# A start offset of 88 instead of 192 bytes for split weights that are the stationary side

## The chip, the cores and the metric

The kernel runs on one NeuronCore of a Trainium2 chip. The metric is the device time of one launch in microseconds; lower is better.

## The reference, cut to what matters

One decoder block on 256 tokens of width 1024, in float32. The heavy part is matrix products with large weights:

```python
h = rms_norm(x, g_pre_mix)
proj = h @ w_in          # 1024 x 4256: MoBA q, k, v, MLA latents, 2 x 1024 gate logits
...                      # two attention branches, o_a and o_b
merged = sigmoid(gate_a) * (o_a @ w_branch_a) + sigmoid(gate_b) * (o_b @ w_branch_b)
x = x + rms_norm(merged @ w_out, g_post_mix)
h2 = rms_norm(x, g_pre_mlp)
m = square(relu(h2 @ w_up)) @ w_down      # 1024 -> 4096 -> 1024
x = x + rms_norm(m, g_post_mlp)
```

## The kernel before, in words

Every float32 operand of a large product is split into a high part (`hi`, rounded by ScalarE to the type float32r that TensorE multiplies) and the rest (`lo`, on VectorE: the value minus `hi`). `mm3` (L180 to L185) then makes one product as three matmuls into the same PSUM tile: hi times hi (L182), and the two mixed ones (L185). In a call `nc.tensor.matmul(ps, a, b)` the operand `a` is the stationary side: its 128 columns are first loaded into the array (a row "PEld LDWEIGHTS" in the profile). The operand `b` is the moving side, which is streamed through (a row "PE MATMUL"). The profile names both as out<-moving,stationary. The load for the next matmul runs while the present one streams.

Weights play either part:

- As the **moving** side, 512 columns or so wide, in `a_chunk` (the q, k, v and latent projections), in `mix` (w_out), and in the first four tiles of w_up. There activations are the stationary side.
- As the **stationary** side in `b_tile` and `nope`: 128 columns of a weight are loaded and 256 tokens are streamed. These are the gate logits (`gate_tiles`, names `acc<-xt_hi,whi` and its two companions), part of the MLA projections (`nope`, `acc<-ct_hi,whi`), the two branch projections (`wk<-o_hi,whi`) and w_up from its fifth tile on (`wk<-x_hi,u_hi`).

Each weight block comes from HBM by one DMA on SyncE's queue into a `raw` tile. `halves_of` (first half of the kernel, buffers `whi`, `wlo`) or `split` (MLP, buffers `u_hi`, `u_lo` and others) turn it into `hi` and `lo`. Both functions take a `skew` in bytes. The buffer is 512 bytes longer per partition than the weights need (`ROW // 4` floats), and the weights begin `skew` bytes into it. Callers whose weights become the stationary side pass `SKEW`, all others 0. In the built program every one of these buffers, and the tiles `xt_hi`, `xt_lo`, `ct_hi`, `ct_lo`, `o_hi`, `o_lo`, `x1_hi`, `x1_lo` that are the moving side against them, begins at a multiple of 512 bytes, and so does each 128-column slice of 512 bytes within a block.

TensorE's instructions stand in the order of the program. During the attention part, `weave` puts gate tiles and MLA products between the attention steps. In the MLP, pair i of w_up tiles (48 matmuls of 256 columns) is followed by the w_down products of pair i - 3 (21 or 24 matmuls of 512 columns, where hidden activations `m_hi`, `m_lo` are the stationary side, at skew 0). Buffers for split weights are double in the MLP and five deep before it. In the last two pairs of w_down the `u` buffers are used without a skew, for weights on the moving side.

Of the kernel before, what the change touches and what calls it, by code (L numbers as in the profile page):

```python
# [37 lines left out]
QUOTA_A, QUOTA_B = 1900, 1900  # L38


ROW, SKEW = 512, 192

PLAIN = (0, 5, 10, 14, 15)

# [895 lines left out]
```

## Time and profile before

| | |
|---|---|
| median of 3 runs (lowest to highest) | 364.34 us (364.11 to 364.54) |
| the profiled execution: its time, its span | 365.11 us, 363.4 us |
| TensorE matmul busy | 354.2 us, 97% of the span, 2319 instructions |
| TensorE weight loads busy | 319.0 us, 88% |
| VectorE busy | 297.7 us, 82% |
| ScalarE busy | 247.7 us, 68% |
| mean granted TensorE clock | 0.993 of 2.4 GHz |

The span is the time from the first to the last instruction of the profiled execution; 1.7 us of its time lie around it. Matmuls are pipelined: one that streams 256 columns is recorded as 0.28 us long, yet the next one starts about 0.118 us after it. So what a matmul costs is read from the distance between starts, and not from its own length.

### The profile page before, as it was taken

How to read it: one execution, taken by the hardware profiler on the slowest of the kernel's cores; microseconds unless marked ns; L12 is line 12 of the kernel's file. 1: busy time of each engine (PE TensorE's matmuls, PEld its weight loads, DVE VectorE, ACT ScalarE, POOL GpSimd, SP SyncE). 2: the span in 40 equal slices, each digit the busy share in tenths (PEclk: the TensorE clock that was granted, in tenths of full speed). 3: DMA queues.
4: the chain of work that ended last, by engine and by line, in shares of the span. 5: the costliest groups of instructions: out<-in, count | busy, mean ns of one | idle time of the engine just before them, and what ended most of it. 6: DMA issues, size and time to landing. Idle time of an engine off the chain costs nothing.

```text
span 363.4 us, 6070 instructions
## 1 busy us (share of the span) xinstructions
PE 354.2 (97%) x2319; PEld 319.0 (88%) x2319; DVE 297.7 (82%) x557; ACT 247.7 (68%) x377; POOL 6.1 (2%) x28
## 2 busy tenths in 40 slices
PE   8999999999999999999999999999999999999992
PEld 4899888989989999998888999999999999999881
DVE  3888998885766576795878799998998999989566
ACT  5799779996758755646369977748556777656422
POOL 6000000000000000000000000000000000000000
PEclk9999999999999999999999999999999999999997
DMA  7987872455333355528804656446755655530002
GB/s 266 336 346 258 262 267 91 147 202 175 119 114 119 115 175 185 190 90 341 347 8 133 223 224 215 178 188 231 250 213 199 239 170 206 231 117 0 2 0 115
DMA packets 14604, 66.20 MB, mean 182 GB/s; under 512 B 1648, under 2 KB 1776, under 8 KB 10480
## 3 DMA queue, kind: packets, MB, share of 16 engines
q1 hardware_dynamic: 14256, 65.30, 50.8%
q10 hardware_dynamic: 288, 0.52, 0.4%
q8 instruction: 18, 0.29, 0.3%
q14 instruction: 10, 0.08, 0.1%
q0 software_dynamic: 32, 0.00, 0.0%
HBM read 64.77 MB, written 1.05 MB: 181 GB/s over the span
## 4 chain that ended last, share of the span: by engine, by line
PE 89%; ACT 5%; DVE 3%; DMA 1%; issue 0%; SPq 0%; DVEq 0%; ACTq 0%
PE acc L185 30%; PE wk L185 25%; PE acc L182 15%; PE wk L182 13%; PE wk L367 2%; PE wk L488 1%; DMA raw<-in_weights 1%; ACT u_hi L655 1%; PE wk L520 1%; ACT sq L243 1%; DVE u_lo L656 1%; DVE y L898 1%; ACT x_sb L779 1%; PE wk L489 1%; ACT t_hi L655 0%; PE wk L519 0%
## 5 line engine op out<-in xcount | busy, mean ns | idle before, releaser
L177 DVE TENSOR_TENSOR wlo<-raw,whi 128x1024 fp32r<-128x1024 f32 (+4 forms) x60 | 66.4, 1107 | 16.9 <-ACT whi L177 16.8
L177 ACT ACTIVATE whi<-raw 128x1024 fp32r<-128x1024 f32 (+4 forms) x60 | 57.4, 965 | 24.7 <-PE acc L185 11.5
L185 PE MATMUL wk<-x_hi,u_lo 128*128 128x256 f32 x224 | 62.7, 280 | 0.0
L182 PE MATMUL wk<-x_hi,u_hi 128*128 128x256 f32 x224 | 62.6, 279 | 0.0
L185 PE MATMUL wk<-x_lo,u_hi 128*128 128x256 f32 x224 | 62.5, 279 | 0.0
L185 PEld LDWEIGHTS wk<-x_lo,u_hi 128*128 128x128 f32 x224 | 42.1, 188 | 0.5
L182 PEld LDWEIGHTS wk<-x_hi,u_hi 128*128 128x128 f32 x224 | 41.9, 187 | 0.5
L185 PEld LDWEIGHTS wk<-x_hi,u_lo 128*128 128x128 f32 x224 | 42.0, 188 | 0.0
L655 ACT ACTIVATE u_hi<-raw_u 128x2048 fp32r<-128x2048 f32 (+1 forms) x17 | 31.0, 1826 | 14.1 <-PE wk L185 13.9
L656 DVE TENSOR_TENSOR u_lo<-raw_u,u_hi 128x2048 fp32r<-128x2048 f32 (+1 forms) x17 | 36.8, 2163 | 4.3 <-ACT u_hi L655 4.3
L182 PE MATMUL acc<-xt_hi,whi 128*128 128x256 f32 x128 | 37.4, 293 | 0.0
L185 PE MATMUL acc<-xt_hi,wlo 128*128 128x256 f32 x128 | 35.7, 279 | 0.0
L185 PE MATMUL acc<-xt_lo,whi 128*128 128x256 f32 x128 | 35.7, 279 | 0.0
L805 ACT ACTIVATE m_hi<-m 128x896 fp32r<-128x896 f32 (+1 forms) x16 | 14.7, 927 | 23.5 <-DVE m L801 21.1
L656 DVE TENSOR_TENSOR t_lo<-t,t_hi 128x2048 fp32r<-128x2048 f32 x11 | 25.2, 2291 | 3.9 <-ACT t_hi L655 3.9
L655 ACT ACTIVATE t_hi<-t 128x2048 fp32r<-128x2048 f32 x11 | 21.1, 1916 | 5.7 <-DVE t L843 5.7
L182 PEld LDWEIGHTS acc<-xt_hi,whi 128*128 128x128 f32 x128 | 24.0, 188 | 1.1 <-issue 1.0
L185 PEld LDWEIGHTS acc<-xt_lo,whi 128*128 128x128 f32 x128 | 24.0, 188 | 0.1
L185 PEld LDWEIGHTS acc<-xt_hi,wlo 128*128 128x128 f32 x128 | 24.0, 188 | 0.0
L656 DVE TENSOR_TENSOR b_lo<-raw_d,b_hi 128x1536 fp32r<-128x1536 f32 x11 | 19.3, 1753 | 0.0
L185 PE MATMUL acc<-t_hi,m_lo 128*128 128x512 f32 x46 | 18.0, 392 | 0.5 <-DVE m_lo L806 0.5
L182 PE MATMUL acc<-t_hi,m_hi 128*128 128x512 f32 x46 | 17.9, 390 | 0.0
(254 smaller groups left out, 925.6 us busy)
## 6 DMA issues: line engine op xcount, KB each, us to landing
raw<-in_weights SPq DMA_DIRECT2D x42, 512.0 KB, 3.4
raw_u<-in_weights SPq DMA_DIRECT2D x17, 1024.0 KB, 4.9
raw_d<-in_weights SPq DMA_DIRECT2D x15, 1024.0 KB, 5.3
raw<-in_weights SPq DMA_DIRECT2D x14, 384.0 KB, 4.6
x_sb<-in_x SPq DMA_DIRECT2D x2, 512.0 KB, 7.0
g_post<-in_g_post SPq DMA_DIRECT2D x2, 512.0 KB, 5.4
raw<-in_weights SPq DMA_DIRECT2D x2, 432.0 KB, 8.1
out<-y SPq DMA_DIRECT2D x2, 256.0 KB, 2.0
```

The costliest lines, as they stand in the source:

```text
L177: last_split[:] = nc.scalar.activation(hi, raw, AF.Copy), nc.vector.tensor_tensor(lo, raw, hi, op=OP.subtract)
L182: nc.tensor.matmul(ps, a_hi, b_hi, start=first, stop=False)
L185: nc.tensor.matmul(ps, a, b, start=False, stop=last and i == 1)
L243: return nc.scalar.activation(sq[:, :src.shape[-1]], src, AF.Square, scale=scale, accum_out=accum)
L367: nc.tensor.transpose(ps[:n, i * P:(i + 1) * P], b, ident)
L488: nc.tensor.matmul(o[:, 0:S], v_of(0, h), pts[h][:, 0:S], start=True, stop=False)
L489: nc.tensor.matmul(o[:, P:S], v_of(1, h), pts[h][:, S:S + P], start=False, stop=True)
L520: nc.tensor.matmul(sp[:, P:3 * P], q[:, P:2 * P], k, start=True, stop=True)
L655: ops = nc.scalar.activation(hi[:, c], src[:, c], AF.Copy), \
L656: nc.vector.tensor_tensor(lo[:, c], src[:, c], hi[:, c], op=OP.subtract)
L779: nc.scalar.activation(x_sb[:, t], x_sb[:, t], AF.Copy, scale=unit_inv[:, t:t + 1])
L805: nc.scalar.activation(hi, m[:, used], AF.Copy)
```

## The change

One constant is changed. Hi and lo weights that are the stationary side begin 88 instead of 192 bytes into their buffers. Buffer sizes and places, the order and the number of instructions on every engine, and all DMAs stay as they are. What differs is the start address of the ScalarE and VectorE writes of those halves, and of the weight loads that read them.

```diff
-ROW, SKEW = 512, 192
+ROW, SKEW = 512, 88
```

The lines that use it, unchanged:

```python
hi, lo = (wts.tile([P, UNIT + ROW // 4], F32R, name=n, tag=n)[:, skew // 4:skew // 4 + raw.shape[-1]]
          for n in ("whi", "wlo"))                                        # L175, in halves_of
hi = mlp(f"{tag}h").tile([P, size], F32R, ...)[:, skew // 4:skew // 4 + n]  # L651, in split; L652 for lo
```

## Rows read from the trace of the kernel before

**Rows 1.** The page's head: busy time by engine with its share of the span, and the chain of work that ended last, by engine.

```profile
span 363.4 us, 6070 instructions
PE 354.2 (97%) x2319; PEld 319.0 (88%) x2319; DVE 297.7 (82%) x557; ACT 247.7 (68%) x377; POOL 6.1 (2%) x28
PE 89%; ACT 5%; DVE 3%; DMA 1%; issue 0%; SPq 0%; DVEq 0%; ACTq 0%
```

**Rows 2.** Matmuls by line and operands, in the view of groups that keeps shapes apart: count, busy us, mean ns of one. These are the matmuls whose stationary side begins at the skew: w_up, gates, branch projections, MLA projections. Each stands for three groups of the same count.

```profile
L182 PE MATMUL wk<-x_hi,u_hi 128*128 128x256 f32 x224 | 62.6, 279 | 0.0
...
L182 PE MATMUL acc<-xt_hi,whi 128*128 128x256 f32 x128 | 37.4, 293 | 0.0
...
L182 PE MATMUL wk<-o_hi,whi 128*128 128x256 f32 x64 | 17.9, 280 | 0.0
...
L182 PE MATMUL acc<-ct_hi,whi 128*128 128x256 f32 x20 | 5.9, 293 | 0.0
```

**Rows 3.** The timeline of TensorE: start us, length us, engine, line, operands. First and last of a run of 48 matmuls of one w_up pair, and the first of what follows.

```profile
213.97 0.28 PE L182 MATMUL wk<-x_hi,u_hi 128*128 128x256 f32 x1
214.08 0.28 PE L185 MATMUL wk<-x_lo,u_hi 128*128 128x256 f32 x1
...
219.50 0.28 PE L185 MATMUL wk<-x_hi,u_lo 128*128 128x256 f32 x1
219.62 0.40 PE L182 MATMUL wk<-b_hi,m_hi 128*128 128x512 f32 x1
```

**Rows 4.** The same view, of a run of 330 matmuls (gates and branch projections) without a pause: the second, the last, and what follows; 329 distances lie between the first row and the last.

```profile
122.12 0.28 PE L185 MATMUL acc<-xt_lo,whi 128*128 128x256 f32 x1
...
160.76 0.28 PE L185 MATMUL wk<-o_hi,wlo 128*128 128x256 f32 x1
160.87 0.40 PE L182 MATMUL acc<-whi,mg_hi 128*128 128x512 f32 x1
```

**Rows 5.** The same view, of three shorter runs of the same kind of matmul. Between the rows of each piece lie 9, 15 and 15 distances.

```profile
62.25 0.28 PE L185 MATMUL acc<-ct_hi,wlo 128*128 128x256 f32 x1
...
63.27 0.28 PE L185 MATMUL acc<-ct_hi,wlo 128*128 128x256 f32 x1
...
89.93 0.28 PE L185 MATMUL acc<-xt_hi,wlo 128*128 128x256 f32 x1
...
91.63 0.28 PE L185 MATMUL acc<-xt_hi,wlo 128*128 128x256 f32 x1
...
119.19 0.28 PE L185 MATMUL acc<-xt_hi,wlo 128*128 128x256 f32 x1
...
120.89 0.28 PE L185 MATMUL acc<-xt_hi,wlo 128*128 128x256 f32 x1
```

**Rows 6.** The same view, of matmuls of 256 columns whose stationary side (hidden activations `m`) begins at a multiple of 512 bytes, as the moving side does. 21 distances lie between the two rows.

```profile
353.52 0.28 PE L185 MATMUL wk<-u_lo,m_hi 128*128 128x256 f32 x1
...
356.04 0.28 PE L185 MATMUL wk<-u_lo,m_hi 128*128 128x256 f32 x1
```

**Rows 7.** The same view, of matmuls of 512 columns with the same start of both sides; 17 distances lie between the two rows.

```profile
341.05 0.39 PE L182 MATMUL acc<-b_hi,m_hi 128*128 128x512 f32 x1
...
344.90 0.39 PE L185 MATMUL acc<-t_lo,m_hi 128*128 128x512 f32 x1
```

**Rows 8.** One piece of the chain of work that ended last: start us, length us, and eight transposes (128 columns loaded and 128 streamed each).

```profile
43.29 0.87 PE wk L367 x8
```

**Rows 9.** The timeline of weight loads in one of the runs of rows 5: start us, length us.

```profile
89.94 0.19 PEld L182 LDWEIGHTS acc<-xt_hi,whi 128*128 128x128 f32 x1
90.05 0.19 PEld L185 LDWEIGHTS acc<-xt_lo,whi 128*128 128x128 f32 x1
```

**Rows 10.** Busy us of each engine in stretches (length, then engine busy and count, granted clock, DMA share, GB/s).

```profile
60.00:122.00 62.00, 62.00 (x494) 56.41 (x492) 45.52 (x137) 50.45 (x120) 0.00 (x0) 1.00 0.42 138
122.00:162.00 40.00, 40.00 (x335) 39.81 (x336) 29.88 (x41) 22.60 (x33) 0.00 (x0) 1.00 0.50 162
208.00:340.00 132.00, 131.51 (x857) 120.37 (x857) 124.16 (x126) 88.26 (x77) 0.00 (x0) 1.00 0.51 184
234.80:245.20 10.40, 10.40 (x70) 9.59 (x69) 10.33 (x10) 5.20 (x5) 0.00 (x0) 1.00 0.49 197
```

**Rows 11.** Waits between 208 and 340 us: who waited for whom, us in total, times, longest.

```profile
ACT u_hi L655 <- PE wk L185: 13.9, 8, 3.6
DVE u_lo L656 <- ACT u_hi L655: 3.2, 3, 1.8
DVE m_lo L806 <- ACT m_hi L805: 0.5, 1, 0.5
```

**Rows 12.** Lines 257 and 258, ScalarE and VectorE reading 256 floats from `raw` (at its start) or from `front` (37 floats into the tile): duration ns min/median/max.

```profile
L257 ACT ACTIVATE xt_hi<-raw,front x7: 500/510/513, 6.5 to 12.1; 128x256 fp32r<-128x256 f32 x7
L257 ACT ACTIVATE xt_hi<-front x1: 507/507/507, 3.1 to 3.1; 128x256 fp32r<-128x256 f32 x1
L258 DVE SCALAR_TENSOR_TENSOR xt_lo<-raw,front,xt_hi x7: 478/481/483, 7.0 to 13.1; 128x256 fp32r<-128x256 f32 x7
L258 DVE SCALAR_TENSOR_TENSOR xt_lo<-front,xt_hi x1: 483/483/483, 3.6 to 3.6; 128x256 fp32r<-128x256 f32 x1
```

## The prediction

> **What bounds the kernel now.** I read the page's head first: TensorE's matmuls are busy for 97% of the span, and 89% of the chain that ended last is theirs [rows 1]. The stretches say the same where the change acts: TensorE is busy 62.00 of 62.00 us, 40.00 of 40.00 and 131.51 of 132.00 [rows 10]. So time per matmul is time of the kernel, unless another engine steps in behind it.
>
> Next I counted the matmuls that the change touches, in the view of groups. The four kinds stand three times each: 3 x (224 + 128 + 64 + 20) = 1308 of 2319 matmuls [rows 2]. Their recorded length of 279 ns is no price, since they overlap. The price is the distance between starts, so the timeline comes third. One w_up pair takes 219.62 - 213.97 = 5.65 us for 48, which is 117.7 ns each [rows 3]; the long run of gates and branch projections takes 160.87 - 122.12 = 38.75 us for 329, which is 117.8 ns [rows 4]. 1308 x 117.8 ns = 154 us, 42% of the span. One nanosecond on each is 1.3 us. The measurement of this kernel can tell about 0.2%, or 0.7 us, from no change; that is 0.55 ns per matmul.
>
> **What the start of the stationary side does to that distance, as far as the trace shows it.** Three prices stand in this one profile, all for 256 streamed columns at the full granted clock:
>
> - 120.0 ns where the stationary side begins at a multiple of 512 bytes: 2.52 us for 21 distances [rows 6].
> - 117.7 to 117.8 ns at 192 bytes, in nearly all runs [rows 3, 4].
> - 113.3 ns, also at 192 bytes, in three short runs: 1.02 us for 9, 1.70 us for 15, 1.70 us for 15 [rows 5].
>
> With 512 columns the distance is 3.85 us for 17, or 226.5 ns [rows 7]. So 256 more columns cost 226.5 - 120.0 = 106.5 ns, which is pure streaming. What a matmul pays beyond that is 13.5 ns without a skew, 11.2 ns in the usual state at 192 bytes, and 6.8 ns in the better one. A load starts with each matmul and runs while it streams: a matmul starts at 89.93 us, a load at 89.94 [rows 5, 9]. I read the extra as the load and the stream getting into each other's way, by an amount that hangs on where the two stand relative to each other. That the same addresses give 117.7 in one run and 113.3 in another, each kept for a whole run, says that a small shift at a run's entry is enough to change it. That the load is what disturbs the stream is my inference; the prices are measured.
>
> **The change part by part.** It removes and adds no instruction and moves none, on any engine or queue. Three things get another start address.
>
> *The writes of hi and lo* by ScalarE and VectorE begin 88 bytes into the buffer. No row shows a write at such a place. The nearest are reads of 256 floats that begin 37 floats (148 bytes) into a tile: 507 ns against 510 at a tile's start on ScalarE, 483 against 481 on VectorE [rows 12]. I take nothing, with a bound of 3 ns either way on each of the 41 splits that have the skew (27 before the MLP, 14 of w_up) on each of two engines, 0.2 us, most of it beside TensorE's work.
>
> *The weight loads* read from there. The price per matmul can lie anywhere that the extra can. Below: the extra falls towards nothing until the load itself is the limit. Eight transposes, which load 128 columns but stream only 128, take 0.87 us, or 108.8 ns each [rows 8]; so 109 ns is the floor. Above: 120.0 ns, the price without a skew. A load of 512 bytes that begins 88 bytes in also covers nine pieces of 64 bytes instead of eight, where 192 covers eight; if the extra goes by pieces, the top is 106.5 + 13.5 x 9/8 = 121.7 ns. The present price lies near the upper end of the span from 109 to 121.7: two thirds of it lie below 117.7. A shift of the load against the stream, which 88 bytes surely is, is therefore more likely to lower the price than to raise it. As the value I take 113.3 ns, the one better state that this trace shows.
>
> *The sum.* Of the 1308, some 45 already run at 113.3 (the three runs of [rows 5] have 12, 17 and 16) and about 20 open a stretch after a wait and have another price. 1243 x (117.75 - 113.3) ns = 5.5 us less. From the profiled execution's 365.11 us (span 363.4 and 1.7 around it) that gives 359.6; it lies 0.8 us above the median of 364.34, so the median should be 358.8 us, 1.5% less.
>
> *Does the gain arrive?* In the MLP, VectorE is the cover that could run out. Between 208 and 340 us it is busy 124.16 of 132.00 us, and 576 touched matmuls lie there (three groups of 192), worth 2.6 us; 129.4 us would remain, and VectorE's work still fits. Locally it is tight: one pair has VectorE busy 10.33 of 10.40 us [rows 10], while that pair would shrink by 48 x 4.45 ns = 0.21 us. What saves it is the lead: the split of the next weights waits for TensorE to give its buffer free, 13.9 us in 8 waits of up to 3.6 us, whereas TensorE's stationary activations were late by 0.5 us once [rows 11]. Four such pairs in a row use up 0.6 us or so of that lead. If the lead were gone, the MLP's 2.6 us would shrink to about 1 us and the time would be 360.4. Before 162 us VectorE and ScalarE have 10 us or more to spare in each stretch [rows 10].
>
> The Trainium skill, in "SBUF — State Buffer", section "A bandwidth-pool intuition that's wrong (but worth ruling out)", gives TensorE a second, independent read port for weight loads. By that the load and the stream never meet, and the start address would change nothing: 364.3 us. The trace does not agree: 120.0 and 117.7 ns differ by the start alone [rows 3, 6].
>
> **The rivals.**
>
> *Nothing changes: 364.3 us.* If only the piece of some hundred bytes in which the load begins decides, or the state is set at each run's entry by what came before, 88 bytes could give the same mixture of 117.7 and 113.3. For it: over all the MLP runs the price is the same although the buffers stand at different places. Against it: the step from 0 to 192 bytes did move the price by 2.3 ns, and 0.55 ns would be seen.
>
> *Slower: the load meets the stream as often as without a skew, or more.* The price goes to 120.0 ns: 1243 x 2.25 ns + 45 x 6.7 ns = 3.1 us more, 367.4 us. With the ninth piece, at 121.7 ns, it is 1243 x 3.95 + 45 x 8.4 = 5.3 us more, 369.6. The place is every run of rows 3 and 4; it decides as soon as the price passes 118.3 ns. For it: 88 bytes is no multiple of 16, 32 or 64, while 0 and 192, whose prices are known, are; and it lies nearer to 0, the bad start, than 192 does. Against it: 120.0 is only 2.3 ns above today's price, so there is little room upwards.
>
> The Trainium skill's same page, section "Door 1: The DMA port swizzle (why `[64,N]` ≈ `[32,N]`)", tells of 16-byte lines and of a penalty for each access that crosses to a new one. A load from byte 88 touches 33 such lines and one from 192 touches 32; by that rule this rival holds, at an estimated 11.2/32 = 0.35 ns per matmul, or 364.8 us. No row here begins a load inside such a line, so nothing yet bears it out.
>
> *Much faster: the extra nearly vanishes.* At 109 ns, 1243 x 8.75 + 45 x 4.3 ns = 11.1 us less, 353.3 us. VectorE's cover in the MLP would then be used up (576 x 8.75 = 5.0 us of a slack of 7.8, with no lead left), so I expect 354 to 355 rather than that.
>
> **How the numbers follow.** The better state, 113 ns or near it: 0.40, with a range of its own from 356.5 to 362 (115.9 to 111.5 ns). Much faster: 0.13. No change: 0.14. Slower: 0.33, mostly up to 368. So faster by over 0.2% has 0.53, within 0.2% 0.14, slower 0.33. For the range I leave out the outer half of "much faster" and the tail of "slower" past 368: 354.5 to 368.0.
>
> **What would show it.** Right: the distances in the w_up runs (48 in 5.65 us before) become 48 in 5.44 us, the run of 330 shrinks from 38.75 to 37.3 us, the groups of `u_hi`, `whi` drop from 279 to 276 ns, and VectorE's busy time stays at 298 us. The 120.0 and 226.5 ns of rows 6 and 7 stay, since their starts do. Wrong: distances of 118.3 ns or more; or distances that drop while TensorE gets new waits for `u_lo` or `m_lo` in the MLP; or splits on ScalarE and VectorE that take longer than before.

## The result and the profile after

The changed kernel takes 361.9 us (median of 6 runs, 361.2 to 362.5) against 364.49 us for the kernel before beside it. The ratio is 0.9924, 95% interval 0.991 to 0.9938: 2.6 us faster, where 5.5 us were forecast (358.8 from 364.34). The direction was right; less than half of the size came, and the time lies inside the stated range.

The head of the page after, which answers to [rows 1]: span, then busy time by engine.

```profile
span 360.7 us, 6070 instructions
PE 351.2 (97%) x2319; PEld 315.8 (88%) x2319; DVE 297.6 (82%) x557; ACT 248.1 (69%) x377; POOL 6.1 (2%) x28
```

TensorE's busy time falls by 3.0 us, the span by 2.7; the other engines do what they did. The groups of [rows 2], after:

```profile
L182 PE MATMUL wk<-x_hi,u_hi 128*128 128x256 f32 x224 | 62.2, 278 | 0.0
...
L182 PE MATMUL acc<-xt_hi,whi 128*128 128x256 f32 x128 | 37.4, 292 | 0.0
...
L182 PE MATMUL wk<-o_hi,whi 128*128 128x256 f32 x64 | 17.9, 279 | 0.0
```

The w_up group shrinks by 1 ns on the mean, and the others hardly. The timeline of TensorE (start us, length us, engine, line, operands) shows where they differ. First the run of 48 w_up matmuls that answers to [rows 3]:

```profile
213.41 0.28 PE L182 MATMUL wk<-x_hi,u_hi 128*128 128x256 f32 x1
213.53 0.28 PE L185 MATMUL wk<-x_lo,u_hi 128*128 128x256 f32 x1
213.64 0.28 PE L185 MATMUL wk<-x_hi,u_lo 128*128 128x256 f32 x1
213.76 0.28 PE L182 MATMUL wk<-x_hi,u_hi 128*128 128x256 f32 x1
213.88 0.28 PE L185 MATMUL wk<-x_lo,u_hi 128*128 128x256 f32 x1
...
218.75 0.28 PE L185 MATMUL wk<-x_hi,u_lo 128*128 128x256 f32 x1
218.87 0.40 PE L182 MATMUL wk<-b_hi,m_hi 128*128 128x512 f32 x1
```

218.87 - 213.41 = 5.46 us for 48, where it was 5.65. The first four distances are still 0.12 us; from the fifth on, 113.3 ns: (218.75 - 213.88)/43. Now the run of 330 gates and branch projections that answers to [rows 4], its second, its last and what follows:

```profile
121.98 0.28 PE L185 MATMUL acc<-xt_lo,whi 128*128 128x256 f32 x1
...
160.25 0.28 PE L185 MATMUL wk<-o_hi,wlo 128*128 128x256 f32 x1
160.37 0.40 PE L182 MATMUL acc<-whi,mg_hi 128*128 128x512 f32 x1
```

38.39 us for 329 is 116.7 ns. It fell by 1.1 ns, not by 4.5. And the first run of w_up matmuls after the transposes of L866, 72 of them, takes a third price:

```profile
198.72 0.28 PE L185 MATMUL wk<-x_lo,u_hi 128*128 128x256 f32 x1
...
207.12 0.28 PE L185 MATMUL wk<-x_hi,u_lo 128*128 128x256 f32 x1
207.24 0.40 PE L182 MATMUL acc<-t_hi,m_hi 128*128 128x512 f32 x1
```

8.52 us for 71 is 120.0 ns, where it was 117.8. So at 88 bytes the same kind of matmul costs 113.3, 116.7 or 120.0 ns, each kept through a run, at a granted clock of 1.00. Summed from starts over all 1308 touched matmuls, waits at the heads of runs included:

| runs of touched matmuls | before, us | after, us | change | forecast |
|---|---|---|---|---|
| 12 runs of 48 (w_up) | 67.81 | 65.53 | -2.28 | -2.56 |
| one of 72, one of 24 (w_up) | 11.39 | 11.46 | +0.07 | -0.43 |
| one of 330 (gates, branches) | 38.97 | 38.61 | -0.36 | -1.47 |
| 19 short ones (306 matmuls, among attention) | 37.86 | 37.49 | -0.37 | -1.07 |
| sum, before rounding | 156.04 | 153.09 | -2.95 | -5.5 |

The forecast column is the prediction's 4.45 ns for each matmul it counted, laid out over the runs.

### The profile page after: what moved, and what is told of

Its sections match the earlier page's. It is cut to its first block, busy times and chain, and to the rows that moved or that the text cites. A ratio compares the mean times of both kernels' runs of the same rounds, so it can differ in the third digit from the quotient of the medians.

```text
span 360.7 us, 6070 instructions
## 1 busy us (share of the span) xinstructions
PE 351.2 (97%) x2319; PEld 315.8 (88%) x2319; DVE 297.6 (82%) x557; ACT 248.1 (69%) x377; POOL 6.1 (2%) x28
## 4 chain that ended last, share of the span: by engine, by line
PE 87%; ACT 5%; DVE 4%; DMA 1%; issue 1%; SPq 0%; DVEq 0%; ACTq 0%
PE acc L185 29%; PE wk L185 25%; PE acc L182 15%; PE wk L182 13%; PE wk L367 2%; PE wk L488 1%; ACT u_hi L655 1%; DMA raw<-in_weights 1%; PE wk L520 1%; ACT sq L243 1%; DVE u_lo L656 1%; DVE y L898 1%; ACT x_sb L779 1%; DVE wlo L177 1%; PE wk L489 1%
## 5 line engine op out<-in xcount | busy, mean ns | idle before, releaser
L182 PE MATMUL wk<-x_hi,u_hi 128*128 128x256 f32 x224 | 62.2, 278 | 0.0
L185 PE MATMUL wk<-x_hi,u_lo 128*128 128x256 f32 x224 | 62.1, 277 | 0.0
L185 PE MATMUL wk<-x_lo,u_hi 128*128 128x256 f32 x224 | 62.0, 277 | 0.0
L182 PEld LDWEIGHTS wk<-x_hi,u_hi 128*128 128x128 f32 x224 | 42.1, 188 | 0.5
L185 PEld LDWEIGHTS wk<-x_lo,u_hi 128*128 128x128 f32 x224 | 42.1, 188 | 0.5
L185 PEld LDWEIGHTS wk<-x_hi,u_lo 128*128 128x128 f32 x224 | 42.0, 188 | 0.0
L182 PE MATMUL acc<-xt_hi,whi 128*128 128x256 f32 x128 | 37.4, 292 | 0.0
L185 PE MATMUL acc<-xt_hi,wlo 128*128 128x256 f32 x128 | 35.6, 278 | 0.0
L185 PE MATMUL acc<-xt_lo,whi 128*128 128x256 f32 x128 | 35.6, 278 | 0.0
L182 PEld LDWEIGHTS acc<-xt_hi,whi 128*128 128x128 f32 x128 | 24.1, 188 | 1.1 <-issue 1.0
L185 PEld LDWEIGHTS acc<-xt_lo,whi 128*128 128x128 f32 x128 | 24.1, 188 | 0.1
L185 PEld LDWEIGHTS acc<-xt_hi,wlo 128*128 128x128 f32 x128 | 24.0, 188 | 0.0
L185 PE MATMUL acc<-t_hi,m_lo 128*128 128x512 f32 x46 | 18.0, 392 | 0.4 <-DVE m_lo L806 0.4
L182 PE MATMUL acc<-t_hi,m_hi 128*128 128x512 f32 x46 | 17.9, 390 | 0.0
```

Of the source, the lines that this page charges most:

```text
L182: nc.tensor.matmul(ps, a_hi, b_hi, start=first, stop=False)
L185: nc.tensor.matmul(ps, a, b, start=False, stop=last and i == 1)
```

## The experiments

Theory A, formed from the trace after: the price of a matmul is one of a few states. A run of like matmuls falls into one of them within its first few, by how it is entered, and stays there. The start offset decides which states there are and which one a given entry leads to. Rivals: the gain is spread evenly (B); the offset's place in 64 bytes or in 512 decides alone (C); the dear runs are dear because of their own operands and buffers (D); or the entry alone decides, at any offset (E). In the scans below the lines stand one further down, L183 and L186 for L182 and L185.

**Only the MLP at 88 bytes.**

```diff
-        w = split(load(f"up{2 * i}", "u"), "u", behind, max(len(behind), 1), SKEW)
+        w = split(load(f"up{2 * i}", "u"), "u", behind, max(len(behind), 1), 88)
```

> Only the w_up pairs of the MLP begin at 88 bytes; gates, branch and MLA projections keep 192. Theory A (the price per matmul is a state that is set where a run of matmuls begins, and the start offset only decides which states there are): the twelve runs of 48 w_up matmuls take 5.46 us each as in the changed kernel (5.65 before), the run of 72 stays at 120 ns or falls into another state, and the long run of gates and branches is back at 117.8 ns; together 2.0 to 2.5 us less than before, ratio 0.993 to 0.995. Rival B (the gain is spread evenly over all touched matmuls, about 2.3 ns each): 672 of 1308 matmuls give half of the 2.6 us, ratio 0.9965.

Ratio 0.9948 (0.993 to 0.9966). All twelve runs of 48 take 5.46 us, the run of 72 stays at 120.0 ns, and the run of 330 is back at 117.8 ns.

**Only the part before the MLP at 88 bytes.**

```diff
-ROW, SKEW = 512, 192
+ROW, SKEW = 512, 88
...
-        w = split(load(f"up{2 * i}", "u"), "u", behind, max(len(behind), 1), SKEW)
+        w = split(load(f"up{2 * i}", "u"), "u", behind, max(len(behind), 1), 192)
```

> The other half: gates, branch and MLA projections begin at 88 bytes, the w_up pairs keep 192. Theory A: the w_up runs are back at 5.65 us, the long run of 330 matmuls stays near 116.7 ns or falls into one of the other states seen at 88 bytes (113.3 or 120), and the whole is 0.4 to 1.0 us faster than before, ratio 0.997 to 0.999. Rival B: half of the gain, ratio 0.9965.

Ratio 0.9983 (0.9974 to 0.9993). The w_up runs are back at 5.65 us, the run of 330 is at 116.7 ns. The two halves add up: 0.52% and 0.17% for 0.76% together, within their intervals. B falls: its ratio of 0.9965 for either half lies outside the second interval (just inside the first), and the distances are not spread evenly, 4.0 ns less per matmul in the w_up runs and 1.1 in the run of 330.

**A price for each offset: three scans.** The twelve w_up runs of 48 are all entered alike, after w_down matmuls of 512 columns, and give the same time to 0.01 us. So each can carry an offset of its own, and one kernel prices twelve.

```diff
+SCAN = (0, 64, 128, 192, 256, 320, 384, 448, 24, 88, 152, 216)
...
-        w = split(load(f"up{2 * i}", "u"), "u", behind, max(len(behind), 1), SKEW)
+        w = split(load(f"up{2 * i}", "u"), "u", behind, max(len(behind), 1), SCAN[i - 4] if i >= 4 else SKEW)
```

> Everything at 192 bytes but the twelve w_up pairs 4 to 15, which begin at 0, 64, 128, 192, 256, 320, 384, 448, 24, 88, 152, 216 bytes in this order, one offset for a pair. All are entered alike, after w_down matmuls of 512 columns, so that each run of 48 gives the price of its offset. Theory A with a period of 64 bytes: the first eight do not differ in their states, and 24, 88, 152 and 216 all settle at 113.3 ns. Theory C (the place within 512 bytes counts, as the step from 0 to 192 suggests): 0 is 120 ns, 192 is 117.7, 88 is 113.3 after a few matmuls, and 24, 152 and 216 differ from 88. Within either, the 192 pair must give 5.65 us and the 88 pair 5.46.

> As the scan before, with 8, 16, 32, 40, 48, 56, 72, 80, 96, 104, 112, 120 bytes for the pairs 4 to 15. If the place within 16-byte lines matters (one more line for a load that begins inside one), 8, 40, 56, 72, 104 and 120 are dearer than their neighbours 16, 32, 48, 80, 96 and 112. If only the distance between load and stream matters, the price is smooth or jumps between the few states seen so far (113.3, 116.7, 117.8, 120 ns), whatever the offset within 16 bytes.

> The twelve w_up pairs 4 to 15 begin at 4, 12, 68, 76, 84, 92, 100, 136, 168, 232, 264, 344 bytes. The scans so far: 0 and 256, 64 and 320, 128 and 384, 192 and 448 agree in pairs, so that a period of 256 bytes predicts 264 as 8 (5.56 us) and 344 as 88 (5.46 us). If 88 is the bottom of a smooth valley, 84 and 92 lie at 113 to 116 ns; if the states jump, they are as dear as 80 and 96 (118.6 and 117.4 ns).

Four of the 36 runs, as the timeline has them: first matmul and the one that follows the run, at 0, 88, 76 and 84 bytes. The first two stand in the first scan, the others in the third. The three kernels took 364.78, 365.01 and 364.51 us, one run each.

```profile
212.93 0.28 PE L183 MATMUL wk<-x_hi,u_hi 128*128 128x256 f32 x1
...
218.69 0.40 PE L183 MATMUL wk<-b_hi,m_hi 128*128 128x512 f32 x1
...
308.17 0.28 PE L183 MATMUL wk<-x_hi,u_hi 128*128 128x256 f32 x1
...
313.63 0.40 PE L183 MATMUL acc<-t_hi,m_hi 128*128 128x512 f32 x1
```

```profile
244.60 0.28 PE L183 MATMUL wk<-x_hi,u_hi 128*128 128x256 f32 x1
...
250.05 0.40 PE L183 MATMUL wk<-b_hi,m_hi 128*128 128x512 f32 x1
...
254.85 0.28 PE L183 MATMUL wk<-x_hi,u_hi 128*128 128x256 f32 x1
...
260.61 0.39 PE L183 MATMUL acc<-t_hi,m_hi 128*128 128x512 f32 x1
```

5.76, 5.46, 5.45 and 5.76 us for 48. All of them, as us for the run of 48, from the starts to 0.01 us:

| offsets in bytes | us for 48 |
|---|---|
| 0, 256 | 5.75, 5.75 |
| 64, 320, 192, 448 | 5.65, 5.65, 5.65, 5.65 |
| 128, 384 | 5.77, 5.77 |
| 24, 152, 216 | 5.83, 5.60, 5.74 |
| 88, 344 | 5.46, 5.46 |
| 8, 264 | 5.56, 5.56 |
| 16, 32, 48, 80, 96, 112 | 5.68, 5.68, 5.68, 5.69, 5.63, 5.75 |
| 40, 56, 72, 104, 120 | 5.71, 5.65, 5.68, 5.65, 5.72 |
| 4, 12, 68, 76, 84, 92, 100 | 5.67, 5.61, 5.68, 5.45, 5.76, 5.68, 5.75 |
| 136, 168, 232 | 5.66, 5.76, 5.68 |

Offsets 256 bytes apart give the same, in all six pairs. Within 256 bytes there is no slope to follow: 76 and 88 are the cheapest, and 80, 84 and 92 beside them cost 5.68 to 5.76. C falls in its form of 64 bytes (24 and 88 differ by 0.37 us), and its 512 bytes are 256. That the offset decides alone fell already with the runs of 330 and 72, which have other prices at the same 88 bytes. Beginning inside a 16-byte piece is no mark of a dear offset: 8, 76 and 88 do so and are the cheapest.

Theory A's few states are too simple. At 0, 64, 76, 88, 192 and 216 bytes the distances become even, within about 1 ns of their mean, but at most of the other offsets they go round in a cycle: 112 and 121 ns in turn at 12 bytes, 118, 118 and 124 at 100. At 24 bytes a cycle of seven runs from 117 to 131 ns; a piece of it from the first scan:

```profile
300.71 0.29 PE L186 MATMUL wk<-x_hi,u_lo 128*128 128x256 f32 x1
300.84 0.30 PE L183 MATMUL wk<-x_hi,u_hi 128*128 128x256 f32 x1
300.97 0.28 PE L186 MATMUL wk<-x_lo,u_hi 128*128 128x256 f32 x1
301.09 0.28 PE L186 MATMUL wk<-x_hi,u_lo 128*128 128x256 f32 x1
301.21 0.28 PE L183 MATMUL wk<-x_hi,u_hi 128*128 128x256 f32 x1
```

The mean of a cycle can lie elsewhere than the states, 115.5 ns at 8 bytes and 118.3 at 16. A pattern, even or in a cycle, then stays to the end of the run.

**The entry changed, the addresses kept.** Two matmuls of 512 columns are put in, one at the head of the branch projections, one ahead of the run of 72.

```diff
+        if m == 0: nc.tensor.matmul(ps, o_hi[:, 0, 0, :P], flat(o_hi[:, 0, 0:2]), start=True, stop=True)
...
+            if i == WARM // 2 and j:
+                nc.tensor.matmul(acc_tile(), x1_hi[:, 0, :P], flat(x1_hi[:, 0:2]), start=True, stop=True)
```

> The changed kernel with two matmuls more: each streams 512 columns over a stationary side that begins at a multiple of 512 bytes, as the w_down matmuls do ahead of every w_up run, and writes a tile that is written over or not read. One stands at the head of the branch projections, inside the run of 330 matmuls at 116.7 ns; the other ahead of the run of 72 w_up matmuls at 120 ns. No address of the others changes. Theory A (the state is set by how a run is entered): both runs settle at 113.3 ns; some 310 x 3.3 + 70 x 6.7 ns = 1.5 us less for 2 x 0.23 us more, so about 1.0 us faster than the changed kernel, ratio to the kernel before 0.989 to 0.990. Rival D (these runs are dearer because of their own operands and buffers): 116.7 and 120 ns stay, the kernel is 0.5 us slower than the changed one, ratio 0.994.

The timeline of this kernel around the two:

```profile
123.70 0.39 PE L623 MATMUL wk<-o_hi 128*128 128x512 f32 x1
123.93 0.28 PE L182 MATMUL wk<-o_hi,whi 128*128 128x256 f32 x1
...
159.30 0.40 PE L182 MATMUL acc<-whi,mg_hi 128*128 128x512 f32 x1
```

```profile
197.48 0.48 PE L864 MATMUL acc<-x_hi 128*128 128x512 f32 x1
197.80 0.28 PE L182 MATMUL wk<-x_hi,u_hi 128*128 128x256 f32 x1
...
205.96 0.40 PE L182 MATMUL acc<-t_hi,m_hi 128*128 128x512 f32 x1
```

35.37 us for 312 and 8.16 us for 72: 113.4 ns each, where the same matmuls at the same addresses took 116.7 and 120.0. D falls. The kernel takes 361.15 us, ratio 0.9896 (0.9879 to 0.9912). Beside it on the same chip the changed kernel was run again:

> The changed kernel once more, beside the others on the same chip: ratio 0.991 to 0.994, w_up runs of 5.46 us, the run of 330 at 116.7 ns and that of 72 at 120 ns if the states are the same in every execution.

361.69 us, ratio 0.9915 (0.9901 to 0.993). Its states are those of the first execution: 5.46 us, 38.60 us for the run of 330, 120.0 ns in the run of 72. From the first gate of the long run to w_out it is 37.80 us with the extra matmul against 38.61 (121.50 to 159.30, 121.14 to 159.75), and 8.48 against 8.72 in the run of 72, extra matmul included: 1.0 us less, as expected. In the medians 0.5 us of it shows. The two intervals do not tell that from nothing; all four times of this kernel lie below all four of the other, by as little as 0.04 us.

**The same entry at 192 bytes.**

```diff
-ROW, SKEW = 512, 88
+ROW, SKEW = 512, 192
```

> The kernel before (192 bytes) with the same two extra matmuls as in the entry experiment. Theory A: the offset decides which price a run takes after such an entry, 113.3 ns at 88 bytes and 117.8 ns at 192, so both runs stay at 117.8 ns and the kernel is 0.5 us slower than before. Rival E (the entry alone does it, whatever the offset): the run of 312 and the run of 72 settle at 113.3 ns at 192 bytes too, 1.7 us less.

Both runs stay where they were, as the row of what follows shows against the start of the run of 312 (123.58 us): 36.75 us, 117.8 ns. The run of 72 is at 117.7 ns, the one time 364.52 us. E falls: in these two runs offset and entry decide together.

```profile
123.58 0.28 PE L182 MATMUL wk<-o_hi,whi 128*128 128x256 f32 x1
...
160.33 0.40 PE L182 MATMUL acc<-whi,mg_hi 128*128 128x512 f32 x1
```

**The moving side shifted instead.**

```diff
-    x1_hi = keep.tile([P, KD, S], F32R, name="x1_hi", tag="xt_hi")
+    x1_hi = keep.tile([P, KD * S + 128], F32R, name="x1_hi", tag="xt_hi")[:, 106:106 + KD * S].rearrange("p (k s) -> p k s", s=S)
...
-        w = split(load(f"up{2 * i}", "u"), "u", behind, max(len(behind), 1), SKEW)
+        w = split(load(f"up{2 * i}", "u"), "u", behind, max(len(behind), 1), 0)
```

(`x1_lo` alike; `xt_hi` and `xt_lo` keep their start in buffers of the same new size, and the `u` buffers lose their 512 bytes more.)

> The kernel before, but in the MLP the w_up weights begin at 0 and the moving side x1_hi, x1_lo begins 424 bytes (minus 88, modulo 512) into its buffer, so that the distance between load and stream is that of the changed kernel while the load begins at a multiple of 512 bytes. If only the distance between the two counts, the runs of 48 settle at 113.3 ns (5.46 us). If the place of the load by itself counts, they stay at 120 ns (5.75 us), as 0 bytes gave in the scan. Another price between 113 and 122 ns would say that both places count.

The first run of 48 and the row that follows it:

```profile
213.90 0.28 PE L182 MATMUL wk<-x_hi,u_hi 128*128 128x256 f32 x1
...
219.65 0.39 PE L182 MATMUL wk<-b_hi,m_hi 128*128 128x512 f32 x1
```

All twelve runs of 48 take 5.76 us, 120.0 ns settled, as an offset of 0 with an unshifted moving side does; the one time is 366.24 us, against 364.86 for the kernel before. So the distance between the two sides alone does not set the price: the place of the load counts by itself at this entry. It is one place of the moving side, and whether its start matters while the load begins at 88 bytes was not tried.

**The offset on matmuls of 512 columns.** On top of the entry experiment, the stationary activations of w_out begin at 88 bytes.

```diff
-    mg_hi = late.tile([P, KD, S], F32R, name="mg_hi", tag="m0")
+    mg_hi = late.tile([P, KD * S + 128], F32R, name="mg_hi", tag="m0")[:, 22:22 + KD * S].rearrange("p (k s) -> p k s", s=S)
```

(`mg_lo` alike.)

> The entry experiment (88 bytes, two extra matmuls) with one thing more: the stationary side of the 96 matmuls of w_out (mg_hi, mg_lo), which stream 512 columns, begins 88 bytes into its buffer. If the extra of 13.3 ns belongs to the load's place also where it has twice the time, their distance falls from 226.7 ns to about 220 ns, 0.6 us less in all, ratio to the kernel before about 0.988. If the extra is another thing with 512 columns, it stays at 226.7 ns and the ratio at 0.9896.

The timeline of w_out in this kernel:

```profile
162.63 0.39 PE L182 MATMUL acc<-whi,mg_hi 128*128 128x512 f32 x1
...
175.93 0.39 PE L182 MATMUL acc<-whi,mg_hi 128*128 128x512 f32 x1
```

13.30 us for 57 is 233.3 ns, against 226.7 before: dearer by 6.6 ns, so neither of the two expected outcomes. Ratio 0.9918 (0.9904 to 0.9932). An offset that is among the cheapest for 256 columns is dearer than 0 for 512. The run of 72, behind the same extra matmul, also took 116.7 ns here instead of 113.3: the matmul just ahead of a run does not settle its state alone.

**76 bytes everywhere.**

```diff
-ROW, SKEW = 512, 192
+ROW, SKEW = 512, 76
```

> All stationary split weights begin at 76 bytes, which in the scan settled at 113.3 ns like 88. The w_up runs of 48 take 5.45 us. Theory A says nothing certain of the run of 330 and the run of 72, which are entered otherwise: each takes one of a few prices between 113.3 and 120 ns, and it need not be the one that 88 bytes takes there (116.7 and 120). If it does take 113.3 in both: ratio 0.988; if 120 in both: 0.995.

360.23 us, ratio 0.989 (0.9872 to 0.9908). The same kernel once more, with more runs:

> 76 bytes once more with more rounds. If the states repeat as they did at 88 bytes: the run of 330 at 113.3 ns (37.5 us with its head), the w_up runs at 5.45 us, ratio to the kernel before 0.988 to 0.990, below the interval of the changed kernel (0.9901 to 0.993).

360.77 us, ratio 0.9899 (0.9881 to 0.9918), with the same times in every run of matmuls to 0.02 us. The first execution's page head, long run and first run of 48:

```profile
span 358.6 us, 6070 instructions
PE 348.9 (97%) x2319; PEld 313.4 (87%) x2319; DVE 297.3 (83%) x557; ACT 248.1 (69%) x377; POOL 6.1 (2%) x28
```

```profile
120.99 0.28 PE L185 MATMUL acc<-xt_lo,whi 128*128 128x256 f32 x1
...
158.28 0.40 PE L182 MATMUL acc<-whi,mg_hi 128*128 128x512 f32 x1
...
211.32 0.28 PE L182 MATMUL wk<-x_hi,u_hi 128*128 128x256 f32 x1
...
216.78 0.40 PE L182 MATMUL wk<-b_hi,m_hi 128*128 128x512 f32 x1
```

37.29 us for 329 is 113.3 ns, and the run of 72 settles at 113.3 too. At this offset every run of 12 matmuls or more reaches the cheap state, most within two to seven matmuls, whatever its entry. The touched matmuls take 151.1 us against 156.0: 4.9 us less, and about 4 us less in the medians. This version beats the kernel before clearly. It is 0.9 to 1.7 us below the changed kernel's medians; the intervals of the ratios still overlap a little (0.9881 to 0.9918 and 0.9901 to 0.993), while the touched matmuls' own sums, 151.1 and 153.1 us, repeat to 0.04 us in the second trace of either kernel.

## Why the prediction was right or wrong

**What bounds the kernel: right.** 3.0 us less of TensorE gave 2.7 us less of span, and with 76 bytes 5.3 gave 4.8.

**The three prices and what they stand for: half right.** That the start offset moves the distance between matmuls, and that the better state is 113.3 ns, was read rightly: w_up settles there. That the two sides' distance decides was an inference and fell with the shifted moving side, at the one place that was tried. That 120.0 and 117.7 ns differ "by the start alone" did not follow from [rows 3, 6], whose operands differ; the scan shows it, with w_up at 0 and at 192 bytes. That the step from 256 to 512 columns is "pure streaming", 106.5 ns, holds at 0 bytes only: at 88 bytes 512 columns cost 233.3 ns and 256 columns 113.3, a step of 120.0.

**Why 113.3 at 88 bytes: right by luck.** The prediction took 113.3 ns because it was the one better state in the trace, and held a lower price likelier because two thirds of the possible span lay below the present one. Of the 29 other starts modulo 256 that the scans tried, six are cheaper than 192 bytes, three equal it to 0.01 us, and 20 are dearer; only 76 and 88 reach 113.3. Nothing in the rows set 88 apart from these 20.

**The sum: this step failed.** It gave 113.3 ns to all of 1243 matmuls. The prediction had read that each price is kept for a whole run and set at its entry, and then did not carry that into the sum: a run that enters otherwise can land in another state. The run of 330 landed at 116.7 ns (0.36 us won, not 1.47), the run of 72 at 120.0 (0.15 us lost, not 0.32 won), and the short runs won 0.37 us, not 1.07. Even the w_up runs spend four dear distances on the way in, so that 48 take 5.46 us, not 5.44. That is 2.6 us of the 5.5. With the two runs entered as w_up is, the missing part of those two came; with 76 bytes nearly all of it.

**The price of the writes: right.** The splits on `whi` and `u_lo` take the same time after as before, to 4 ns in the medians of over 1000 ns.

**VectorE as cover: right.** Between 208 and 340 us the split of the next weights (ScalarE's `u_hi`, which VectorE's `u_lo` follows) waited less for TensorE to give its buffer free, and TensorE's stationary activations are no later:

```profile
ACT u_hi L655 <- PE wk L185: 9.6, 8, 3.0
DVE u_lo L656 <- ACT u_hi L655: 1.3, 2, 1.1
DVE m_lo L806 <- ACT m_hi L805: 1.4, 2, 0.9
PEld acc L185 <- DVE m_lo L806: 0.8, 1, 0.8
```

The lead fell from 13.9 to 9.6 us [rows 11]. TensorE waits once, for `m_lo` of the first w_down pair: its load waits 0.8 us, up to 208.06 us. The kernel before has the same wait, up to 208.60 us, which [rows 11] do not show:

```profile
PEld acc L185 <- DVE m_lo L806: 0.8, 1, 0.8
PE acc L185 <- DVE m_lo L806: 0.5, 1, 0.5
```

The prediction misread a row there: the 0.5 us of `m_lo` in [rows 11] is VectorE waiting for ScalarE. That TensorE was late by 0.5 us once is true all the same, by the second of these two rows.

**The rivals.** "Nothing changes" and "slower" did not come as a whole, but both came in part: that a state is set at each run's entry belongs to the first, and the 120.0 ns of the run of 72 is the price of the second. The second read port that the Trainium skill's page "SBUF — State Buffer" (section "A bandwidth-pool intuition that's wrong (but worth ruling out)") gives to weight loads does not make the start indifferent here: offsets from 0 to 120 bytes gave 5.45 to 5.83 us for the same 48 matmuls. The rule on 16-byte lines on the Trainium skill's same page (section "Door 1: The DMA port swizzle (why `[64,N]` ≈ `[32,N]`)") did not sort the offsets either: 88 and 76 begin inside such a line and are cheaper than 80 and 96.

**What stays open** is why. The prices, the period of 256 bytes and the part of the entry are measured; what in the chip makes 76 and 88 good and 84 bad is not, and whether a load disturbs a stream was not tried, since no kernel here runs these matmuls without loads.

## What to carry to other kernels

Where matmuls with a fresh stationary side follow each other closely, read their distance from starts, run by run, and not as a mean over a group: a price that repeats in one run and not in the next is a state, and a change will move each run by itself. Price a start offset by a scan, many offsets in one kernel at places that are entered alike, rather than by reasoning from one or two of them. Then check the winner at every kind of entry and width that the kernel has; here 76 bytes reached the cheap state in every run of 12 or more, while 88 reached it behind w_down and in most short runs, but not in the runs of 330 and 72. At 512 columns 76 was not tried.

## What the runs showed of the hardware that was not expected

- Equal matmuls of 256 columns at a granted clock of 1.00 run at 113.3, 116.7, 117.8 or 120.0 ns apart, the first three in runs of 330 without a change. At other starts the distances go round in a cycle that repeats, 117 to 131 ns at 24 bytes.
- The same addresses give different states after different entries (116.7 and 113.4 ns in the branch projections), and the long runs take the same state in both traces of a kernel: 38.61 and 38.60 us for the run of 330 at 88 bytes. One run of 18 differed, by 0.04 us.
- The start of the stationary side counts modulo 256 bytes: six pairs of offsets agree to 0.01 us.
- Twelve bytes (76 to 88) make almost no difference behind w_down (5.45 and 5.46 us for 48) and 3.3 ns per matmul in the run of 330; eight bytes (76 to 84) cost 0.31 us in 48 matmuls.
- With 512 columns, 88 bytes cost 6.6 ns more than 0.
